# First norm of a diffusion layer: all modulation shifts as 2-column products on TensorE, scalings moved from GpSimd to VectorE

## The chip, the core and the metric

One core of a Trainium2 chip runs one layer of a hybrid recurrent backbone. The metric is the device time of one execution in microseconds (us). The engines named below are TensorE (PE in the rows, its weight loads PEld), VectorE (DVE), ScalarE (ACT), GpSimd (POOL) and SyncE (SP), which issues most transfers.

## The reference, cut to what matters

```python
def rmsnorm(x, w):
    y = x * lax.rsqrt(jnp.mean(x * x, axis=-1, keepdims=True) + EPS)
    return y * w
def modulate(xn, shift, scale):
    return xn * (1 + scale) + shift
mod_lat = jnp.split(silu(c) @ w_mod[l] + b_mod[l], N_MOD, axis=-1)
mod_ctx = jnp.split(silu(c_ctx) @ w_mod[l] + b_mod[l], N_MOD, axis=-1)
# first of three blocks; the same for the context tokens with mod_ctx
x = x + 0.5 * gate * swiglu(modulate(rmsnorm(x, norm1_w), shift, scale), ffn1_w1, ffn1_w2)
```

D_MODEL is 1024, there are 512 latent and 256 context tokens, and the hidden width is 2816. The whole layer is in float32. What is changed is the first `modulate(rmsnorm(...))` and its place beside the first products of `ffn1_w1`.

## The kernel before, in words

The activations lie transposed: 8 tiles `xa[k]` of 128 features by 768 tokens (columns 0 to 255 context, 256 to 767 latent). Every product of float32 matrices is made of three products of halves: a rounded high part (`xh`, `whi`) and a remainder (`xl`, `wlo`).

**Statistics.** ScalarE squares the 8 tiles, VectorE adds them, and TensorE sums over the partitions in `rms_sum` with matmuls whose stationary operand is a 128x128 block of squares and whose moving operand is one column of ones (`aux<-ones,six` in the rows). GpSimd takes the power, VectorE spreads it on a diagonal, and TensorE multiplies that with ones, so that the factor R stands in all partitions (`rms_spread`, `aux<-six,ones`).

**Modulation.** For tile k, scale and shift are 128 numbers each for latent and context. A scale is two VectorE reductions `mod_dot` of 128x1024 (one for `c`, one for `c_ctx`; `mod_scr` in the rows), then a small `TENSOR_SCALAR` into `a1`. A shift is one of two things. For tiles 5 and 7 (`SHIFT_V`) it is two more `mod_dot`. For the others it is 8 float32 matmuls on TensorE with the 128x2 `ccol` as stationary and 128 columns of weights as moving operand. This gives a row of 2x128, which ScalarE copies out of PSUM, TensorE transposes (`mm<-ident,row`), and ScalarE adds to the bias (`s1`). A float32 matmul stands in the records as two, so a shift is 16 records.

**Norm of a tile.** `scaled` multiplies the tile with R, on GpSimd for tiles 2, 4 and 6 (`ROOT_P`), on VectorE for the others. `norm_seg` then makes, for latent and context apart, `xh` and the full value in place on ScalarE, and `xl` as their difference on VectorE.

**Products.** `ffn1` makes the first two of 22 hidden tiles (each has a gate and an up half) as the norm proceeds: for each tile k there are four quarters, (hidden tile, half), of 6 matmuls each: three of 512 and three of 256 columns. After each quarter the generator `more(k)` is asked for one step. So what it yields stands between quarters in TensorE's order. TensorE, VectorE, ScalarE and GpSimd each run their instructions in the order written here (`ordered = True`); from the third hidden tile on a scheduler sets the order.

**Transfers.** SP issues in order; `fetch(k)` brings a tile of scale weights (512 KB) and one of shift weights. Shift weights and some `ffn1_w1` tiles share five buffers (`four`).

Of the kernel before, what the change touches and what calls it, by code (L numbers as in the profile page):

```python
# [7 lines left out]
F32 = mybir.dt.float32  # L8
F32R = mybir.dt.float32r
AF = mybir.ActivationFunctionType  # L10
ALU = mybir.AluOpType

P = 128
DM = 1024
KT = DM // P
# [11 lines left out]
CTX, LAT, LAT_A, LAT_B = (0, NC_), (NC_, NL), (NC_, 256), (NC_ + 256, 256)  # L27
ONES = [(m, 1) for m in range(KT)]
FOUR = [(0, 4)] + [(m, 1) for m in range(4, KT)]
CTX_MODS = (0, 1, 2, 3, 4)  # L30

SHIFT_V = (5, 7)
ROOT_P = (2, 4, 6)

# [33 lines left out]
class Space1:  # L70
# [14 lines left out]
    rows = lambda self, j, i: self.x[:, 2 * ((j + 2) % 4) + i, :]  # L85
# [13 lines left out]
class Builder:  # L99
# [1118 lines left out]
    def _build(self, st):  # L1218
        nc, tc, T = self.nc, self.tc, self.T
# [26 lines left out]
        with ExitStack() as f1:  # L1246
            p1 = lambda name, bufs=1, **kw: f1.enter_context(tc.tile_pool(name=name, bufs=bufs, **kw))
            space = self.space = Space1(self, p1("fp1"))
# [5 lines left out]
            xa = [xT[:, k, :] for k in range(KT)]  # L1254
            self.x, self.xc = [t[:, NC_:] for t in xa], [t[:, :NC_] for t in xa]
            crow = [space.quad(F32) for _ in range(2)]
            ccol = self.modp.tile([P, KT, 2], F32, name="ccol")
# [21 lines left out]
            for k in range(KT):  # L1279
                self.sq_add(S, k, xa[k], NT, "vvvvvvlv")()  # L1280
                if k in (0, 1, 3, 5):
                    r, q = parts[(k + 1) // 2]
                    nc.scalar.activation(self.cb[:, r, q * 512:q * 512 + 512], pcs[2 * r + q], AF.Silu)

            pc = self.ps.tile([P, 512], F32, name="mm")
            for _ in range(3):
                nc.tensor.matmul(pc, lhsT=self.ident, rhs=self.cb[:, 0, :512], start=True, stop=True)
            b1 = ct("b1", [P, KT])
            self.ts(b1, self.bmod[:, 1, :], 1.0, ALU.add)
            R = xT[:, KT, :]  # L1290
            a1, s1 = ct("a1", [P, KT, 2]), ct("s1", [P, KT, 2])

            def mod_dot(w, c, dst):
                scr = self.modp.tile([P, DM], mybir.dt.bfloat16, name="mod_scr", bufs=1)
                nc.vector.tensor_tensor_reduce(out=scr, in0=w, in1=self.cb[:, c, :], scale=1.0, scalar=0.0,
                                               op0=ALU.mult, op1=ALU.add, accum_out=dst)

            wms, wss = {}, {}

            def fetch(k):  # L1300
                wms[k] = self.modp.tile([P, DM], F32, name="wm", bufs=2) if k < 2 else self.tmp.tile([P, DM], F32)
                nc.sync.dma_start(out=wms[k], in_=T["w_mod"][KT + k])
                wss[k] = space.quad(F32)
                nc.sync.dma_start(out=wss[k], in_=T["w_mod"][k] if k in SHIFT_V else T["w_shift"][k])

            def shift(k):
                ws = wss.pop(k)
                if k in SHIFT_V:
                    for c in range(2):
                        mod_dot(ws, c, s1[:, k, c:c + 1])  # L1310
                    self.ts(s1[:, k, :], s1[:, k, :], self.bmod[:, 0, k:k + 1], ALU.add)
                    return
                pr = self.ps.tile([P, 512], F32, name="mm") if k < 2 else self.aux.tile([P, 512], F32, name="aux")
                for q in range(KT):
                    nc.tensor.matmul(pr[0:2, 0:P], lhsT=ccol[:, q, :], rhs=ws[:, q * P:(q + 1) * P],
                                     start=(q == 0), stop=(q == KT - 1))
                row = self.modp.tile([2, P], F32, name="row", bufs=2)
                nc.scalar.copy(out=row, in_=pr[0:2, 0:P])
                return row

            def shift_cols(k, row):
                if k in SHIFT_V:
                    return
                pt = self.ps.tile([P, 512], F32, name="mm") if k < 2 else self.aux.tile([P, 512], F32, name="aux")
                nc.tensor.transpose(out=pt[:, 0:2], in_=row, identity=self.ident[0:2, 0:2])
                nc.scalar.activation(s1[:, k, :], pt[:, 0:2], AF.Identity, bias=self.bmod[:, 0, k:k + 1])

            def scale(k):
                wm = wms.pop(k)
                for c in range(2):  # L1330
                    mod_dot(wm, c, a1[:, k, c:c + 1])
                self.ts(a1[:, k, :], a1[:, k, :], b1[:, k:k + 1], ALU.add, self.nw[:, 0, k:k + 1], ALU.mult)

            def norm_seg(k, w):
                lo, n = (LAT, CTX)[w]
                hi, x = self.xh[k][:, lo:lo + n], xa[k][:, lo:lo + n]
                kw = dict(scale=a1[:, k, w:w + 1], bias=s1[:, k, w:w + 1])
                nc.scalar.activation(hi, x, AF.Identity, **kw)
                nc.scalar.activation(x, x, AF.Identity, **kw)
                self.tt(self.xl[k][:, lo:lo + n], x, hi.bitcast(F32), ALU.subtract)  # L1340

            def scaled(k):
                (nc.gpsimd if k in ROOT_P else nc.vector).tensor_tensor(out=xa[k], in0=xa[k], in1=R, op=ALU.mult)

            rows = {}

            def more(k):

                for q in ((1, 2) if k == 0 else (k + 2,)):
                    if q >= KT:  # L1350
                        return
                    if q > 1:
                        if q + 2 < KT:
                            fetch(q + 2)
                        if q + 1 < KT:
                            scaled(q + 1)
                            scale(q + 1)
                    yield lambda: rows.__setitem__(q, shift(q)) if q not in SHIFT_V else None
                    yield lambda: (shift_cols(q, rows.get(q)), norm_seg(q, 0), norm_seg(q, 1),
                                   shift(q + 1) if q + 1 in SHIFT_V else None)  # L1360

            def w_raw(j, half):
                raw = space.quad(F32) if j else self.wp.tile([P, DM], F32, name="wraw", bufs=2)
                hi, lo = ([self.wp.tile([P, DM], F32R, name=n) for n in ("whi", "wlo")] if j + half < 2 else
                          [space.pair() for _ in range(2)])
                nc.sync.dma_start(out=raw, in_=T["f1w1"][j, half])
                return hi, lo, raw

            w_hi = lambda w: nc.scalar.activation(w[0], w[2], AF.Copy)
            w_lo = lambda w: self.tt(w[1], w[2], w[0].bitcast(F32), ALU.subtract)  # L1370
            fetch(0)
            w = [w_raw(0, 0), w_raw(0, 1), w_raw(1, 0), w_raw(1, 1)]
            fetch(1)
            accs = list(S.values())[::-1]
            mod_dot(wms[0], 0, a1[:, 0, 0:1])
            ms = [self.rms_sum([a[:, lo:lo + n] for a in accs], n) for lo, n in (LAT, CTX)]
            w_hi(w[0])
            w_hi(w[1])
            row = shift(0)
            mod_dot(wms[0], 1, a1[:, 0, 1:2])  # L1380
            dg = [self.rms_diag(m) for m in ms]
            self.ts(a1[:, 0, :], a1[:, 0, :], b1[:, 0:1], ALU.add, self.nw[:, 0, 0:1], ALU.mult)
            pR = [self.rms_spread(d) for d in dg]
            shift_cols(0, row)
            w_lo(w[0])
            segs = list(zip((LAT, CTX), pR))
            for (lo, n), r in segs:
                self.tt(xa[0][:, lo:lo + n], xa[0][:, lo:lo + n], r[:, :n], ALU.mult)
            w_lo(w[1])
            norm_seg(0, 0)  # L1390
            w_hi(w[2])
            norm_seg(0, 1)
            for (lo, n), r in segs:
                nc.scalar.copy(out=R[:, lo:lo + n], in_=r[:, :n])
            w_hi(w[3])
            w_lo(w[2])
            scale(1)
            self.tt(xa[1], xa[1], R, ALU.mult)
            w_lo(w[3])
            fetch(2)  # L1400
            fetch(3)
            scaled(2)
            scale(2)
            first = [[x[:2] for x in w[2 * q:2 * q + 2]] for q in range(2)]

            def late():
# [34 lines left out]
            def then(seg, b):  # L1441
                lo, n = seg

                def spill():
                    nc.sync.dma_start(out=xs[:, :, lo - NC_:lo - NC_ + n], in_=self.xT[:, :, lo - NC_:lo - NC_ + n])
                return self.seg_norm(seg, 3, b) + ([spill] if lo >= NC_ else [])
            self.ffn1(space, first, more, hook, mods, ahead, then)
            start = self.mixer_start(box["ws"])
        with ExitStack() as mx:
# [115 lines left out]
```

## Time and profile before

| | us |
|---|---|
| median of 3 runs (lowest to highest) | 1313.13 (1312.42 to 1314.64) |
| the profiled execution, its own time | 1315.44 |
| its span in the trace | 1313.6 |
| busy in it: TensorE, VectorE, ScalarE, GpSimd | 1287.5, 1012.3, 577.8, 56.5 |

The profiled execution's time lies 1.84 us over its span, and 2.31 us over the median of the runs. TensorE is busy 98% of the span. The granted clock of TensorE, PEclk, is given as a share of 2.4 GHz: 1.00 is the full level, 0.50 is 1.2 GHz.

### The profile page before, as it was taken

The numbers are of one execution on the slowest core, as the hardware profiler recorded it, in microseconds if no ns is written. First come the engines' busy times: TensorE is split into PE (matmuls) and PEld (weight loads), VectorE is DVE, ScalarE is ACT, GpSimd is POOL, SyncE is SP. The second block draws the span as 40 slices with busy tenths as digits, with TensorE's granted clock in tenths as the row PEclk, the third lists the DMA queues.
The fourth block names the chain that finished last, engine by engine and source line by source line (L and its number), as shares of the span: only waits on it lengthen the run. The fifth ranks groups of instructions, "written<-read, shape, count | busy, mean of one in ns | idle before, by whom it ended". The sixth has DMA issues, their size and how long they took to land.

```text
span 1313.6 us, 20542 instructions
## 1 busy us (share of the span) xinstructions
PE 1287.5 (98%) x8198; PEld 1180.6 (90%) x8198; DVE 1012.3 (77%) x1621; ACT 577.8 (44%) x992; POOL 56.5 (4%) x81
## 2 busy tenths in 40 slices
PE   8999999999999999999989999999999999999996
PEld 4689999999998888999978798889998999999996
DVE  5995878777779888767677867986578788888866
ACT  5562444444442222383457343444473444444434
POOL 2100000000000000110100000000000000000001
PEclk7999999999999999999989999999999999999998
DMA  8324443434687765413051101115224222233201
GB/s 330 122 88 155 134 150 121 137 136 149 211 279 236 267 212 195 148 44 120 2 146 48 65 33 49 64 49 171 87 99 142 97 96 97 102 108 105 104 17 65
DMA packets 48803, 163.60 MB, mean 125 GB/s; under 512 B 5554, under 2 KB 10034, under 8 KB 48708
## 3 DMA queue, kind: packets, MB, share of 16 engines
q1 hardware_dynamic: 46308, 150.50, 33.5%
q0 software_dynamic: 2400, 11.80, 2.8%
q8 instruction: 64, 1.05, 0.3%
q14 instruction: 31, 0.25, 0.1%
HBM read 149.39 MB, written 12.89 MB: 124 GB/s over the span
## 4 chain that ended last, share of the span: by engine, by line
PE 92%; DVE 3%; ACT 2%; issue 1%; DMA 1%; POOL 0%; SPq 0%; POOLq 0%; DVEq 0%
PE mm L56 71%; PE aux L56 21%; DVE mod_scr L56 1%; DMA x<-in_xT 0%; ACT xh L56 0%; DMA wraw<-in_wo 0%; DVE x L56 0%; ACT six L56 0%; ACT nm_y L56 0%; ACT x L56 0%; DVE wlo L56 0%; DVE xl L56 0%; ACT nm_t L56 0%; ACT whi L56 0%; POOL rms_acc L56 0%
## 5 line engine op out<-in xcount | busy, mean ns | idle before, releaser
L56 PE MATMUL mm<-xh,whi 128*128 128x256 f32 (+2 forms) x1072 | 345.6, 323 | 1.2 <-ACT xh L56 1.2
L56 PE MATMUL mm<-xh,wlo 128*128 128x256 f32 (+2 forms) x1072 | 342.6, 320 | 0.8 <-DVE wlo L56 0.8
L56 PE MATMUL mm<-xl,whi 128*128 128x256 f32 (+2 forms) x1000 | 323.8, 324 | 2.5 <-DVE xl L56 2.5
L56 PEld LDWEIGHTS mm<-xh,whi 128*128 128x128 f32 x1072 | 203.3, 190 | 14.3 <-issue 1.8
L56 PEld LDWEIGHTS mm<-xh,wlo 128*128 128x128 f32 x1072 | 203.5, 190 | 10.8 <-DVE wlo L56 1.0
L56 PE MATMUL mm<-six,whi 128*128 128x384 f32 (+1 forms) x752 | 209.2, 359 | 0.0
L56 PEld LDWEIGHTS mm<-xl,whi 128*128 128x128 f32 x1000 | 189.9, 190 | 14.5 <-DVE xl L56 4.3
L56 ACT ACTIVATE whi<-wraw 128x1024 fp32r<-128x1024 f32 x100 | 106.0, 1062 | 170.1 <-PE aux L56 90.9
L56 PEld LDWEIGHTS mm<-six,whi 128*128 128x128 f32 x752 | 135.6, 188 | 10.0
L56 PE MATMUL mm<-six,wlo 128*128 128x384 f32 (+1 forms) x376 | 134.4, 357 | 0.0
L56 DVE TENSOR_TENSOR wlo<-wraw,whi 128x1024 fp32r<-128x1024 f32 x100 | 121.8, 1220 | 10.5 <-ACT whi L56 10.4
L56 DVE CUSTOM_DVE_ANT_0 mod_scr<-wm,cb 128x1024 bf16<-128x1024 f32 x84 | 105.4, 1255 | 2.2 <-DMA wm<-in_w_mod 2.0
L56 PEld LDWEIGHTS mm<-six,wlo 128*128 128x128 f32 x376 | 70.6, 188 | 6.5
L56 DVE SCALAR_TENSOR_TENSOR x<-mm,mod_l,x 128x256 f32<-128x256 f32 (+1 forms) x88 | 51.9, 601 | 18.4 <-PE mm L56 18.3
L56 PE MATMUL aux<-ah,w2hi 128*128 128x512 f32 x160 | 64.1, 401 | 0.0
L56 ACT ACTIVATE whi<-four 128x1024 fp32r<-128x1024 f32 x37 | 39.2, 1061 | 56.1 <-PE mm L56 49.0
L56 PE MATMUL aux<-al,w2hi 128*128 128x512 f32 x160 | 63.1, 395 | 0.0
L56 DVE SCALAR_TENSOR_TENSOR x<-aux,mod_l,x 128x512 f32<-128x512 f32 x80 | 59.0, 745 | 5.2 <-PE aux L56 5.2
L56 DVE TENSOR_TENSOR wlo<-four,whi 128x1024 fp32r<-128x1024 f32 x37 | 45.3, 1224 | 22.7 <-ACT whi L56 22.7
L56 PE MATMUL aux<-ah,w2lo 128*128 128x512 f32 x160 | 62.4, 390 | 0.0
L56 PE MATMUL mm<-tl,whi 128*128 128x256 f32 x216 | 61.1, 283 | 0.0
L56 PE MATMUL aux<-six,whi 128*128 128x256 f32 x320 | 59.0, 282 | 0.0
(334 smaller groups left out, 2555.1 us busy)
## 6 DMA issues: line engine op xcount, KB each, us to landing
wraw<-in_f1w SPq DMA_DIRECT2D x62, 512.0 KB, 4.0
wm<-in_w_mod SPq DMA_DIRECT2D x58, 512.0 KB, 4.3
wraw<-in_f2w SPq DMA_DIRECT2D x44, 512.0 KB, 3.3
wraw<-in_wi SPq DMA_DIRECT2D x32, 512.0 KB, 3.3
w2raw<-in_f2w SPq DMA_DIRECT2D x22, 512.0 KB, 4.5
four<-h SPq DMA_DIRECT2D x22, 384.0 KB, 5.2
h<-x POOLq DMA_DIRECT2D x18, 384.0 KB, 3.0
wraw<-in_wo SPq DMA_DIRECT2D x8, 512.0 KB, 4.5
```

Of the source, the lines that this page charges most:

```text
L56: r = f(*a, **kw)
```

## The change

`SHIFT_V` and `ROOT_P` go. All eight shifts are made on TensorE with the operands exchanged: a 128x128 block of the weights is stationary and `ccol` moves, 2 columns wide. The result is already a column per partition, so the row, its copy and its transpose go. The shifts of tiles 1 to 7 stand between the quarters of tiles 0 and 1. All scalings with R are on VectorE. The dots of the next tile stand in front of each `xl`, which is one 768-column instruction from tile 1 on. A `keep_busy` of 4 idle matmuls (before: 3) stands ahead of the statistics, and another of 2 behind `rms_spread`. The order of the transfers changes with it.

```diff
-            pc = self.ps.tile([P, 512], F32, name="mm")
-            for _ in range(3):
-                nc.tensor.matmul(pc, lhsT=self.ident, rhs=self.cb[:, 0, :512], start=True, stop=True)
+            idle = self.ps.tile([P, 512], F32, name="mm")
+            def keep_busy(n):
+                for _ in range(n):
+                    nc.tensor.matmul(idle, lhsT=self.ident, rhs=self.cb[:, 0, :512], start=True, stop=True)
+            keep_busy(4)
...
             def shift(k):
                 ws = wss.pop(k)
-                if k in SHIFT_V:
-                    for c in range(2):
-                        mod_dot(ws, c, s1[:, k, c:c + 1])
-                    self.ts(s1[:, k, :], s1[:, k, :], self.bmod[:, 0, k:k + 1], ALU.add)
-                    return
-                pr = self.ps.tile([P, 512], F32, name="mm") if k < 2 else self.aux.tile([P, 512], F32, name="aux")
+                pr = self.aux.tile([P, 512], F32, name="aux")
                 for q in range(KT):
-                    nc.tensor.matmul(pr[0:2, 0:P], lhsT=ccol[:, q, :], rhs=ws[:, q * P:(q + 1) * P],
+                    nc.tensor.matmul(pr[:, 0:2], lhsT=ws[:, q * P:(q + 1) * P], rhs=ccol[:, q, :],
                                      start=(q == 0), stop=(q == KT - 1))
-                row = self.modp.tile([2, P], F32, name="row", bufs=2)
-                nc.scalar.copy(out=row, in_=pr[0:2, 0:P])
-                return row
...
+                nc.scalar.activation(s1[:, k, :], pr[:, 0:2], AF.Identity, bias=self.bmod[:, 0, k:k + 1])
...
+            def norm(k):
+                for out in (self.xh[k], xa[k]):
+                    for w in range(2):
+                        norm_act(k, w, out)
+                self.tt(self.xl[k], xa[k], self.xh[k].bitcast(F32), ALU.subtract)
...
             def scaled(k):
-                (nc.gpsimd if k in ROOT_P else nc.vector).tensor_tensor(out=xa[k], in0=xa[k], in1=R, op=ALU.mult)
+                self.tt(xa[k], xa[k], R, ALU.mult)
...
             def more(k):
...
+                q = k + 2
+                if k == 0:
+                    yield lambda: (shift(1), norm(1))
+                    yield lambda: (scaled(2), scale(2), fetch_shift(6), shift(2))
+                    yield lambda: (scaled(3), scale(3), norm(2), fetch_shift(7), shift(3))
+                    yield lambda: shift(4)
+                    return
+                if q + 1 < KT:
+                    scaled(q + 1)
+                    scale(q + 1)
+                if k == 1:
+                    yield lambda: shift(5)
+                    yield lambda: (norm(q), shift(6))
+                    yield lambda: shift(7)
+                elif q < KT:
+                    yield lambda: norm(q)
...
             pR = [self.rms_spread(d) for d in dg]
-            shift_cols(0, row)
+            keep_busy(2)
+            fetch(2)
+            fetch_shift(3)
+            fetch(3)
             w_lo(w[0])
+            mod_dot(wms[1], 0, a1[:, 1, 0:1])
```

The first place is TensorE beside the products of tile 0. In the names `xh,whi` is a moving and a stationary operand, `two` a weight half of the second hidden tile, `aux` and `mm` are PSUM banks. Before, the third quarter stands between a transpose and the shift of tile 2:

```order
L56 MATMUL mm<-ident,row 128x2
L56 MATMUL mm<-xh,whi 128x512
L56 MATMUL mm<-xl,whi 128x512
L56 MATMUL mm<-xh,wlo 128x512
L56 MATMUL aux<-xh,whi 128x256
L56 MATMUL aux<-xl,whi 128x256
L56 MATMUL aux<-xh,wlo 128x256
L56 MATMUL aux<-four,ccol 2x128 x8
```

Now it stands between two shifts with 2 moving columns, and so does each of the seven quarters from the second on:

```order
L53 MATMUL aux<-ccol,four 128x2 x8
L53 MATMUL mm<-xh,whi 128x512
L53 MATMUL mm<-xl,whi 128x512
L53 MATMUL mm<-xh,wlo 128x512
L53 MATMUL aux<-xh,whi 128x256
L53 MATMUL aux<-xl,whi 128x256
L53 MATMUL aux<-xh,wlo 128x256
L53 MATMUL aux<-ccol,four 128x2 x8
L53 MATMUL mm<-xh,two 128x512
```

The second place is VectorE ahead of the first product. `x<-x,aux` is tile 0 times R, `wlo` the low part of a weight, and the two rows named ISA are a dot and the reading of its sum. Before, the scaling of tile 0 follows the first `wlo`:

```order
L56 TENSOR_TENSOR wlo<-wraw,whi 128x1024
L56 TENSOR_TENSOR x<-x,aux 128x512
L56 TENSOR_TENSOR x<-x,aux 128x256
L56 TENSOR_TENSOR wlo<-wraw,whi 128x1024
L56 TENSOR_TENSOR xl<-x,xh 128x512
```

Now a dot of tile 1's scale weights (`wm`) stands in front of it:

```order
L53 TENSOR_TENSOR wlo<-wraw,whi 128x1024
L53 ISA mod_scr,a_155<-wm,cb 128x1024
L53 ISA a_155 128x1
L53 TENSOR_TENSOR x<-x,aux 128x512
L53 TENSOR_TENSOR x<-x,aux 128x256
L53 TENSOR_TENSOR wlo<-wraw,whi 128x1024
```

The dot came from behind `xl` of tile 0. From the third hidden tile on the engines' orders are those of before, apart from a few neighbours on VectorE and ScalarE that changed places.

## Rows read from the trace of the kernel before

**Rows 1.** The page, part 4: the chain that ended last, by engine.
```profile
PE 92%; DVE 3%; ACT 2%; issue 1%; DMA 1%; POOL 0%; SPq 0%; POOLq 0%; DVEq 0%
```
**Rows 2.** TensorE's timeline: start us, us, engine, line, what, count [wait].
```profile
25.02 0.49 PE L56 MATMUL mm<-xh,whi 128*128 128x512 f32 x1 [1.20 <-ACT xh L56]
...
28.40 0.58 PE L56 MATMUL mm<-xl,whi 128*128 128x256 f32 x1 [0.36 <-DVE xl L56]
...
51.31 1.91 PE L56 MATMUL aux<-four,ccol 128*2 128x128 f32 x16
...
54.39 0.22 PE L56 MATMUL aux<-ident,row 2*128 2x2 f32 x1
...
56.74 0.40 PE L56 MATMUL mm<-xh,whi 128*128 128x512 f32 x1
...
57.79 0.40 PE L56 MATMUL mm<-xh,whi 128*128 128x512 f32 x1
...
60.95 0.40 PE L56 MATMUL mm<-xh,whi 128*128 128x512 f32 x1
...
80.25 0.48 PE L56 MATMUL mm<-xh,six 128*128 128x512 f32 x1
```
**Rows 3.** VectorE and GpSimd from 28 to 47 us, timelines of each.
```profile
28.71 7.95 POOL L56 TENSOR_TENSOR x<-x 128x768 f32<-128x768 f32 x3 [8.58 <-ACT x L56]
...
29.40 2.83 DVE L56 CUSTOM_DVE_ANT_0 mod_scr<-wm,cb 128x1024 bf16<-128x1024 f32 x1
...
42.27 0.95 DVE L56 TENSOR_TENSOR x<-x 128x768 f32<-128x768 f32 x1
43.13 1.22 DVE L56 CUSTOM_DVE_ANT_0 mod_scr<-six,cb 128x1024 bf16<-128x1024 f32 x1
...
46.79 1.22 DVE L56 CUSTOM_DVE_ANT_0 mod_scr<-six,cb 128x1024 bf16<-128x1024 f32 x1
```
**Rows 4.** ScalarE and VectorE ahead of the first product, timelines of each.
```profile
17.34 1.06 ACT L56 ACTIVATE whi<-wraw 128x1024 fp32r<-128x1024 f32 x1 [3.20 <-DMA wraw<-in_f1w]
18.62 1.06 ACT L56 ACTIVATE whi<-wraw 128x1024 fp32r<-128x1024 f32 x1 [0.22 <-DMA wraw<-in_f1w]
...
23.27 1.02 DVE L56 TENSOR_TENSOR x<-x,aux 128x512 f32<-128x512 f32 x2 [1.36 <-PE aux L56]
```
**Rows 5.** Stretches: from:to, length, busy us of each engine, PEclk, DMA share, GB/s.
```profile
13.50:15.70 2.20, 1.51 (x14) 1.43 (x13) 1.53 (x3) 0.63 (x1) 0.00 (x0) 1.00 1.03 412
15.80:18.10 2.30, 2.30 (x12) 2.30 (x12) 0.70 (x3) 0.76 (x1) 1.03 (x1) 0.50 1.03 411
18.20:22.50 4.30, 4.30 (x18) 2.34 (x18) 3.64 (x7) 1.50 (x3) 1.61 (x1) 0.50 1.03 410
22.60:25.90 3.30, 1.72 (x6) 0.70 (x4) 2.20 (x4) 1.97 (x4) 0.00 (x0) 1.00 1.02 408
26.10:32.80 6.70, 5.83 (x22) 3.35 (x23) 5.29 (x6) 3.52 (x7) 4.09 (x2) 0.50 0.76 287
46.50:80.20 33.70, 33.70 (x198) 28.09 (x197) 30.36 (x55) 20.56 (x33) 0.00 (x0) 1.00 0.06 18
```
**Rows 6.** TensorE's timeline: PEclk is 0.50 in the first four, then returns (667.7 us).
```profile
15.18 3.07 PE L56 MATMUL aux<-ones,six 128*128 128x1 f32 x16 [0.69 <-DVE six L56]
...
29.12 3.58 PE L56 MATMUL mm<-four,ccol 128*2 128x128 f32 x16
...
664.33 0.41 PE L56 MATMUL mm<-whi,xh 128*128 128x256 f32 x1
664.54 0.41 PE L56 MATMUL mm<-wlo,xh 128*128 128x256 f32 x1
...
667.73 0.28 PE L56 MATMUL mm<-wlo,xh 128*128 128x256 f32 x1
```
**Rows 7.** TensorE's timeline: one-column sums at PEclk 1.00, later in the kernel.
```profile
550.58 1.40 PE L56 MATMUL aux<-ones,rms_acc 128*128 128x1 f32 x12
```
**Rows 8.** The tile `four`, 0 to 80 us: transfers, from issue to landing.
```profile
DMA to landing us min/median/max: 3.3/8.1/10.2
```

More of the change, by code (lines that the diff above doesn't have):

```diff
@@ L30 @@
 CTX_MODS = (0, 1, 2, 3, 4)
-SHIFT_V = (5, 7)
-ROOT_P = (2, 4, 6)
 MIXER = ("iv1 ck0 mq0 vals0 ck1 rows0 cq1 cols0 iv0 vals1 cq0 pair0 pair0 pair0 pair1 prep0 prep0 fin4 scan0 "
@@ L1298, in _build, with fetch, fetch_shift @@
             wms, wss = {}, {}
[L1300 to L1304, printed above, removed]
+            def fetch(*ks):
+                for k in ks:
+                    wms[k] = self.modp.tile([P, DM], F32, name="wm", bufs=2) if k < 2 else self.tmp.tile([P, DM], F32)
+                    nc.sync.dma_start(out=wms[k], in_=T["w_mod"][KT + k])
+            def fetch_shift(*ks):
+                for k in ks:
+                    wss[k] = space.quad(F32)
+                    nc.sync.dma_start(out=wss[k], in_=T["w_shift"][k])
             def shift(k):
                 ws = wss.pop(k)
-                if k in SHIFT_V:
-                    for c in range(2):
-                        mod_dot(ws, c, s1[:, k, c:c + 1])
-                    self.ts(s1[:, k, :], s1[:, k, :], self.bmod[:, 0, k:k + 1], ALU.add)
-                    return
-                pr = self.ps.tile([P, 512], F32, name="mm") if k < 2 else self.aux.tile([P, 512], F32, name="aux")
+                pr = self.aux.tile([P, 512], F32, name="aux")
                 for q in range(KT):
-                    nc.tensor.matmul(pr[0:2, 0:P], lhsT=ccol[:, q, :], rhs=ws[:, q * P:(q + 1) * P],
+                    nc.tensor.matmul(pr[:, 0:2], lhsT=ws[:, q * P:(q + 1) * P], rhs=ccol[:, q, :],
                                      start=(q == 0), stop=(q == KT - 1))
-                row = self.modp.tile([2, P], F32, name="row", bufs=2)
-                nc.scalar.copy(out=row, in_=pr[0:2, 0:P])
-                return row
[L1321 to L1326, printed above, removed]
+                nc.scalar.activation(s1[:, k, :], pr[:, 0:2], AF.Identity, bias=self.bmod[:, 0, k:k + 1])
             def scale(k):
@@ L1332, in scale, with norm_act @@
                 self.ts(a1[:, k, :], a1[:, k, :], b1[:, k:k + 1], ALU.add, self.nw[:, 0, k:k + 1], ALU.mult)
+            def norm_act(k, w, out):
+                lo, n = (LAT, CTX)[w]
+                nc.scalar.activation(out[:, lo:lo + n], xa[k][:, lo:lo + n], AF.Identity, scale=a1[:, k, w:w + 1],
+                                     bias=s1[:, k, w:w + 1])
             def norm_seg(k, w):
                 lo, n = (LAT, CTX)[w]
-                hi, x = self.xh[k][:, lo:lo + n], xa[k][:, lo:lo + n]
@@ L1337, in norm_seg @@
[L1337 to L1340, printed above, removed]
+                norm_act(k, w, self.xh[k])
+                norm_act(k, w, xa[k])
+                self.tt(self.xl[k][:, lo:lo + n], xa[k][:, lo:lo + n], self.xh[k][:, lo:lo + n].bitcast(F32), ALU.subtract)
+            def norm(k):
[3 more added lines that the diff above has]
+                self.tt(self.xl[k], xa[k], self.xh[k].bitcast(F32), ALU.subtract)
@@ L1342, in scaled @@
             def scaled(k):
-                (nc.gpsimd if k in ROOT_P else nc.vector).tensor_tensor(out=xa[k], in0=xa[k], in1=R, op=ALU.mult)
-            rows = {}
+                self.tt(xa[k], xa[k], R, ALU.mult)
             def more(k):
[L1349 to L1360, printed above, removed]
+                q = k + 2
@@ L1371, in _build @@
             fetch(0)
+            fetch_shift(0)
             w = [w_raw(0, 0), w_raw(0, 1), w_raw(1, 0), w_raw(1, 1)]
             fetch(1)
+            fetch_shift(1, 2)
             accs = list(S.values())[::-1]
@@ L1378, in _build @@
             w_hi(w[1])
-            row = shift(0)
+            shift(0)
             mod_dot(wms[0], 1, a1[:, 0, 1:2])
@@ L1388, in _build @@
                 self.tt(xa[0][:, lo:lo + n], xa[0][:, lo:lo + n], r[:, :n], ALU.mult)
+            wms.pop(0)
             w_lo(w[1])
@@ L1395, in _build @@
             w_hi(w[3])
+            mod_dot(wms[1], 1, a1[:, 1, 1:2])
+            wms.pop(1)
+            self.ts(a1[:, 1, :], a1[:, 1, :], b1[:, 1:2], ALU.add, self.nw[:, 0, 1:2], ALU.mult)
+            scaled(1)
             w_lo(w[2])
-            scale(1)
-            self.tt(xa[1], xa[1], R, ALU.mult)
             w_lo(w[3])
[L1400 to L1403, printed above, removed]
+            fetch(4, 5)
+            fetch_shift(4, 5)
+            fetch(6, 7)
             first = [[x[:2] for x in w[2 * q:2 * q + 2]] for q in range(2)]
```

## Prediction

> **What bounds the kernel now.** First the chain of work that ended last: 92% of it is TensorE [rows 1], so a change counts by what it does to TensorE's time. Then TensorE's timeline in the stretch that the change touches. The first product starts at 25.02 us, and the third hidden tile's first product at 80.25 [rows 2]: the stage is 55.2 us long. Behind it the engines' orders are those of before, so I price only this stage. A quarter takes 57.79 - 56.74 = 1.05 us and a tile of four 60.95 - 56.74 = 4.21 [rows 2], so eight tiles are 33.7 us of products. A shift takes 1.9 us and a transpose 0.2 [rows 2]; five of each stand in the stage: 10.5 us. That is 44.2 us of work at the full clock. The other 11 us are waits of tile 0, VectorE's late dots, and stretches at half clock.
>
> Third, the granted clock by stretches, where the reader is to look at PEclk beside the busy column [rows 5]. It is 1.00 in 13.5 to 15.7 us, which holds one-column sums, and 0.50 behind it, although TensorE is busy all of 15.8 to 18.1 with more such sums. It is still 0.50 in 18.2 to 22.5, which holds a shift with 128 moving columns and the wide products that spread R, and 1.00 behind that. It falls again behind 22.6 to 25.9, where TensorE is busy for half the time. At half clock from 26.1 us to 32.8 stands a shift of 128 moving columns, and it is 1.00 after it. From 46.5 us on, with products and such shifts, it stays 1.00.
>
> **The change, part by part.**
>
> *Scalings and dots on VectorE.* While GpSimd scales three tiles (28.71 to 36.66 us), a dot takes 2.83 us; alone it takes 1.22 [rows 3]. Two dots and a small operation are slowed there, about 4.5 us, which goes. The three scalings come to VectorE at 0.95 us each [rows 3], and four dots (tiles 5 and 7), 4.9 us, leave it. None of this is on TensorE's path later on: a tile costs VectorE one scaling, two dots and one difference, from 42.27 to 46.79 us, 4.5 us [rows 3]. That is 0.3 us more than TensorE's 4.21, but seven quarters and seven shifts now stand ahead of tile 2's products, over 20 us, and VectorE needs about 14 for what tile 2 waits for; the lead of 6 us covers six tiles. If that cover were gone, the cost would be 0.3 us a tile.
>
> *Start of the stage.* A dot of tile 1 now stands ahead of tile 0's scaling, which began at 23.27 us [rows 4]. Its weights are the fourth transfer behind the one that landed at 17.34; the next landed at 18.62 [rows 4], so 1.28 us apart, and these land at about 22.5. The dot ends at 23.7, and tile 0's scaling, its norm and the first product queue behind it: 0.4 us later. The last `xl` product of tile 0's first quarter starts at 28.8 instead of 28.40 [rows 2], and the quarter ends at 29.1. The 4 and 2 idle matmuls fall into time in which TensorE waits for these; at half clock the two behind the spreading may delay the first product, but it would wait for `xl` anyway (bounds 0 to 0.5 us, I take 0). ScalarE loses the row copies; VectorE's single 768-column `xl` costs no more than the two.
>
> *Transfers.* On SP the shift weights of tiles 4 and 5 now wait until the shifts of tiles 1 and 2 have read their buffers, and the scale weights of 6 and 7 wait behind them. They are needed three shifts and two or three quarters later, over 6 us at the full clock; a landing takes 3.3 us at best, 8.1 in the crowded start [rows 8]. I take 0, with 2 us as the upper end.
>
> *The shifts, at the full clock.* With the operands exchanged, the nearest rows are the one-column sums: a 128x128 stationary block for hardly any moving columns. Twelve records take 1.40 us [rows 7], so sixteen take 1.9: as much as the old form. So nothing is gained or lost per shift. Seven shifts stand in the stage instead of five (+3.8 us), and five transposes go (-1.0).
>
> *The sum at the full clock.* From 29.1 us: 31 quarters of 1.05 (32.6) and 7 shifts of 1.9 (13.3) end at 75.0, against 80.25: 5.2 us less.
>
> *The shifts and the clock.* Here I choose. From 29 us on TensorE's work is a shift, a quarter, a shift, a quarter, seven times, about two thirds of it shift at the full clock. The old shift kept company with a clock of 1.00, or stood just ahead of its return. The new shift's kin, the one-column sums, stood ahead of a fall and beside a clock that stayed down, with TensorE busy throughout [rows 5]. So I expect the clock to fall early in tile 0 and to be down for most of the fourteen pieces. The Trainium skill ("TensorE: Matmul & The Clock Gate", "What's actually happening") says that the gate follows how busy the engine has been; by it, with no gap in the shifts, the clock holds and the sum is the 5.2 us gain. The one-column stretch, busy 2.30 of 2.30 us at 0.50, speaks against reading "busy" as the profile's column does.
>
> At half clock a 256-column matmul takes 664.54 - 664.33 = 0.21 us [rows 6]. A quarter is 9 such units, 1.9 us, 0.85 over the full clock. A shift: sixteen sums took 3.07 us with the first half microsecond still fast, and the old shift 3.58 [rows 6]; I take 3.5, 1.6 over. A shift and a quarter lose 2.5 us. Bounds: none of the seven pairs, or all of them (17.5). I take six, 15.0 us. Behind them dense products at half clock must first bring the clock back. Where products alone did that, it took from before 664.3 to 667.7 us [rows 6], about 3.5 us, half of it lost: 1.7. The stage ends at 75.0 + 15.0 + 1.7 = 91.7 us, 11.5 later.
>
> The span becomes 1313.6 + 11.5 = 1325.1, with 1.84 around it 1326.9. The median of the runs is 2.31 below the profiled execution, so the forecast is 1324.6 us.
>
> **The rivals.**
>
> *The clock holds.* 1308 us (-5.2). For it: TensorE has no idle time between the pieces, and the idle matmuls stand ahead of them. Against it: the sums of 13.5 to 18.1 us. It decides if the full-speed quarters, a third of the time, are enough to hold 1.00; no stretch here shows that mix. Range 1306 to 1310.
>
> *The clock falls and returns in between.* The quarters at half clock are 1.9 us of every 5.4 and could bring it back for a while. With half the pairs slow: 3.5 x 2.5 = 8.7, without a final wait, less 5.2: 3.5 later, 1316.7 us. For it: wide products did bring it back at 22.6 us and at 667.7. Against it: it took longer dense stretches there. Range 1315 to 1321.
>
> *The change gains and loses the same.* Two pairs at half clock (5.0 us) cancel the gain: 1313 us, for instance if the fall comes only with the last shifts.
>
> **How the numbers follow.** Chances: clock down for most of the stage 0.40 (1321 to 1327), back in parts 0.23, cancelling 0.10, clock holds 0.27. A difference of 0.2%, 2.6 us, is about what this kernel's measurement can tell. So faster 0.27, same 0.10, slower 0.63. The range takes in the holding clock from below, 1307, since it has more than two chances in ten, and nearly all seven pairs from above, 1327.
>
> **What would show it.** In the trace after: PEclk in stretches between 26 and 70 us; the start of tile 2's first product (about 50 us if the clock holds, 65 if it is down); sixteen shift records in 1.9 us or in 3.5; no dot over 1.3 us; `xl` of tile 2 ready by 45 us, well ahead. Wrong would be: the clock stays at 1.00 beside the 2-column shifts, or TensorE waits for shift weights or for VectorE between tiles 1 and 3.

## The result and the profile after

The changed kernel takes 1326.56 us (median of 4 runs, 1324.85 to 1328.5) against 1313.54 before in the same set: ratio 1.0099, 95% interval 1.0085 to 1.0112. It is slower by 13 us; the forecast was 1324.6, in a range of 1307 to 1327.

The page of the profile after shows the loss without a place: TensorE is busy for 98% of the span as before, and only the second of the 40 slices of PEclk has fallen.

```profile
PE 1302.9 (98%) x8230; PEld 1201.6 (91%) x8230; DVE 1005.2 (76%) x1607; ACT 575.1 (43%) x988; POOL 48.7 (4%) x78
...
PEclk8599999999999999999989999999999999999998
```

Before, the last of these lines reads:

```profile
PEclk7999999999999999999989999999999999999998
```

The place is in the stretches (columns as in [rows 5]), cut where the granted clock changes:

```profile
13.20:19.90 6.70, 6.40 (x45) 5.32 (x45) 5.01 (x12) 3.21 (x5) 2.50 (x2) 1.00 1.03 411
20.00:23.30 3.30, 3.30 (x6) 1.69 (x5) 1.98 (x3) 0.00 (x0) 0.00 (x0) 0.50 1.02 408
23.50:26.70 3.20, 1.51 (x4) 0.36 (x2) 2.88 (x6) 2.26 (x3) 0.00 (x0) 1.00 1.03 410
26.90:67.60 40.70, 40.33 (x162) 37.46 (x163) 23.74 (x37) 14.78 (x30) 0.00 (x0) 0.50 0.35 134
67.90:92.30 24.40, 24.40 (x142) 21.39 (x141) 18.05 (x27) 12.34 (x19) 0.00 (x0) 1.00 0.06 22
```

The reader is to see the fourth line: TensorE is busy for 40.33 of 40.70 us, hardly waits, and has 1.2 GHz all that time. The third line is to be seen beside it: the clock fell at about 26.8 us, behind a stretch in which TensorE was busy for 1.51 of 3.20 us, and so ahead of the first of the seven shifts. The kernel before has the same fall at 26.1, and its clock was back at 32.8 [rows 5]. What this profile shows of the shifts is that the clock did not come back beside them; that it also falls beside them is seen in e9_dot_back_2col. TensorE's timeline shows what it does there:

```profile
25.27 0.50 PE L53 MATMUL mm<-xh,whi 128*128 128x512 f32 x1 [0.77 <-ACT xh L53]
...
29.25 3.41 PE L53 MATMUL aux<-ccol,four 128*128 128x2 f32 x16
...
32.51 0.77 PE L53 MATMUL mm<-xh,whi 128*128 128x512 f32 x1
...
34.58 3.41 PE L53 MATMUL aux<-ccol,four 128*128 128x2 f32 x16
...
66.58 0.63 PE L53 MATMUL mm<-xh,whi 128*128 128x512 f32 x1
...
67.81 0.28 PE L53 MATMUL mm<-xh,whi 128*128 128x256 f32 x1
...
92.31 0.46 PE L53 MATMUL mm<-xh,six 128*128 128x512 f32 x1
```

A shift of sixteen records takes 3.41 us and a quarter 34.58 - 32.51 = 2.07. Seven pairs, 5.33 us apart, run from 29.25 to 66.58, where tile 2's products begin. 1.2 us later the clock is back. The third hidden tile's first product comes at 92.31, 12.06 us later than before [rows 2]; the spans differ by 1325.5 - 1313.6 = 11.9. So the whole loss between the two profiles lies in this stage.

VectorE's timeline shows that it is not the cause:

```profile
22.48 1.22 DVE L53 CUSTOM_DVE_ANT_0 mod_scr<-wm,cb 128x1024 bf16<-128x1024 f32 x1 [1.32 <-DMA wm<-in_w_mod]
...
23.63 1.01 DVE L53 TENSOR_TENSOR x<-x,aux 128x512 f32<-128x512 f32 x2
...
43.59 0.95 DVE L53 TENSOR_TENSOR xl<-x,xh 128x768 fp32r<-128x768 f32 x1
...
56.71 0.96 DVE L53 TENSOR_TENSOR xl<-x,xh 128x768 fp32r<-128x768 f32 x1 [8.56 <-ACT x L53]
```

Tile 2's `xl` is ready at 44.5 us, 22 us before TensorE wants it. The long wait of tile 3's `xl` (8.56 us, on ScalarE, whose norms stand in order behind the slow shifts) is harmless: TensorE comes to tile 3 only at about 71.

### The profile page after: what moved, and what is told of

It reads as the page before. It is cut to its first block, busy times and chain, and to the rows that moved or that the text cites. A ratio compares the mean times of both kernels' runs of the same rounds, so it can differ in the third digit from the quotient of the medians.

```text
span 1325.5 us, 20586 instructions
## 1 busy us (share of the span) xinstructions
PE 1302.9 (98%) x8230; PEld 1201.6 (91%) x8230; DVE 1005.2 (76%) x1607; ACT 575.1 (43%) x988; POOL 48.7 (4%) x78
## 4 chain that ended last, share of the span: by engine, by line
PE 92%; ACT 2%; DMA 2%; DVE 2%; issue 1%; SPq 0%; POOL 0%; POOLq 0%; DVEq 0%; ACTq 0%
PE mm L53 70%; PE aux L53 22%; DMA wm<-in_w_mod 1%; DMA x<-in_xT 1%; DMA wraw<-in_wo 1%; ACT xh L53 1%; DVE x L53 0%; ACT nm_y L53 0%; ACT x L53 0%; SPq L1259 0%; ACT nm_t L53 0%; ACT whi L53 0%; DVE wlo L53 0%; POOL rms_acc L53 0%; DVE xl L53 0%
## 5 line engine op out<-in xcount | busy, mean ns | idle before, releaser
L53 DVE CUSTOM_DVE_ANT_0 mod_scr<-wm,cb 128x1024 bf16<-128x1024 f32 x84 | 102.3, 1218 | 2.2 <-DMA wm<-in_w_mod 2.0
```

What stands on the lines that cost most here:

```text
L53: r = f(*a, **kw)
```

## The experiments

Theory A: shifts with two moving columns let the clock fall, or keep it down, for the seven pairs, and without that the change would be a gain. Theory B: two more shifts on TensorE, and the order of the pieces, cost the time. The runs were made in three sets, each with the kernel before beside it: its median was 1312.98 in the first (e1 to e4), 1312.83 in the second (e5 to e8) and 1314.09 in the third (e9 to e11). Ratios are to that median, so runs of different sets are better compared by ratio.

### e1_old_form: the old operands at the new places

```diff
-  nc.tensor.matmul(pr[:, 0:2], lhsT=ws[:, q * P:(q + 1) * P], rhs=ccol[:, q, :], ...)
-  nc.scalar.activation(s1[:, k, :], pr[:, 0:2], ...)
+  nc.tensor.matmul(pr[0:2, 0:P], lhsT=ccol[:, q, :], rhs=ws[:, q * P:(q + 1) * P], ...)
+  nc.scalar.copy(out=rows[k], in_=pr[0:2, 0:P])
+  # cols(k), one quarter later: transpose of rows[k], then the activation into s1
```

> The changed kernel with the shifts' operands as before the change: two stationary columns, 128 moving ones, a row copy and a transpose, one quarter later. All eight stay on TensorE, in the places that the change gave them. Theory A (the clock: sixteen records with two moving columns let it fall, and all else is worth some 5 us): a shift and a quarter take 1.91 + 1.05 us in place of the 5.33 measured, seven pairs give back 16.6 us, less seven transposes of 0.22 (1.5): 1311.5 us, 1309 to 1314, granted clock 1.00 from 33 us on. Theory B (two more shifts on TensorE and the order of the pieces cost the time, whatever the operands): 1326 to 1328.

Measured: 1319.88 us, ratio 1.0052 (1.0035 to 1.0069): between the two, 8 us over theory A's figure. The stretches, ScalarE and TensorE at 40 to 45 us:

```profile
33.20:43.30 10.10, 7.48 (x52) 5.46 (x50) 6.01 (x9) 4.60 (x10) 0.00 (x0) 1.00 0.94 354
43.50:50.10 6.60, 5.53 (x22) 3.59 (x23) 6.42 (x14) 1.54 (x5) 0.00 (x0) 0.50 0.21 81
50.30:85.50 35.20, 35.20 (x216) 29.41 (x214) 25.91 (x35) 19.34 (x34) 0.00 (x0) 1.00 0.05 16
```

```profile
41.87 1.30 ACT L53 ACTIVATE xh<-x,s,a 128x512 fp32r<-128x512 f32 x2 [3.98 <-DVE a L53]
...
44.28 0.24 ACT L53 COPY row<-aux 2x128 f32<-2x128 f32 x1
```

```profile
44.57 0.26 PE L53 MATMUL aux<-ident,row 2*128 2x2 f32 x1 [3.89 <-ACT row L53]
```

The old form brings a wait that the new one does not have. The row copy of shift 3 stands on ScalarE behind tile 2's norm, which waits 3.98 us for VectorE's dots; TensorE's transpose waits 3.89 us for the copy, and within that idle time the clock falls to 0.50, for 6.8 us. On both sides of it, from 33.4 to 43.4 us and from 50.2 on, the clock is at 1.00 beside these shifts. So A is supported, its sum was not: 3.9 of wait and half of 6.8 are 7.3 us that it left out.

### e2_pad128: two columns repeated to 128

```diff
-  nc.tensor.matmul(pr[:, 0:2], lhsT=ws[:, q * P:(q + 1) * P], rhs=ccol[:, q, :], ...)
+  cols = ccol[:, q, :].rearrange("p (o r) -> p o r", o=1).broadcast_to([P, 64, 2])
+  nc.tensor.matmul(pr[:, 0:128].rearrange("p (o r) -> p o r", r=2), lhsT=ws[:, q * P:(q + 1) * P], rhs=cols, ...)
```

> The changed kernel, with the two moving columns of each shift repeated to 128 (the other 126 results are not used). Stationary blocks, places and what follows stay. Theory A in the form 'few moving columns': the clock holds, a shift takes 1.9 to 2.1 us, the seven pairs 7 x 3.0: 1309 us, 1308 to 1312. Theory A in the form 'loads of whole stationary blocks, each used once': the clock falls as before, a shift takes 3.4 to 3.8 us: 1326 to 1330. Theory B (order and number of pieces): 1326 to 1328, with the clock at 1.00 and waits on TensorE in their place.

Measured: 1311.36 us, ratio 0.9991 (0.9981 to 1.0000), 15 us less than the changed kernel (14 by the ratios). Stretches and TensorE:

```profile
28.80:32.10 3.30, 3.30 (x18) 3.30 (x17) 3.26 (x6) 0.85 (x1) 0.00 (x0) 0.50 0.38 150
32.20:76.40 44.20, 43.52 (x284) 39.24 (x283) 38.64 (x58) 24.39 (x42) 0.00 (x0) 1.00 0.29 108
```

```profile
28.83 3.54 PE L53 MATMUL aux<-ccol,four 128*128 128x128 f32 x16
...
33.26 1.95 PE L53 MATMUL aux<-ccol,four 128*128 128x128 f32 x16
...
36.10 1.95 PE L53 MATMUL aux<-ccol,four 128*128 128x128 f32 x16
...
42.60 2.05 PE L53 MATMUL aux<-ccol,four 128*128 128x128 f32 x16 [0.68 <-ACT s L53]
```

Same stationary blocks, same places, same number of records: only the moving columns differ, and the clock, down when the first shift starts, is back at its end (32.2 us) and stays. That excludes theory B, and it excludes the weight loads alone as the cause. Against the kernel before, the gain is 1.6 us, and the interval of its ratio reaches 1.0000.

### e3_spread: the same shifts, one to a tile

```diff
   yield lambda: (shift(1), norm(1))
-  yield lambda: (scaled(2), scale(2), fetch_shift(6), shift(2))
-  yield lambda: (scaled(3), scale(3), norm(2), fetch_shift(7), shift(3))
-  yield lambda: shift(4)
+  yield lambda: (scaled(2), scale(2), fetch_shift(6))
+  yield lambda: (scaled(3), scale(3), shift(2), norm(2), fetch_shift(7))
...
-  if k == 1:
-      yield lambda: shift(5)
-      yield lambda: (norm(q), shift(6))
-      yield lambda: shift(7)
-  elif q < KT:
-      yield lambda: norm(q)
+  if q < KT:
+      yield lambda: (shift(q), norm(q))
```

> The changed kernel with two shifts in tile 0 and one in each later tile, operands as changed: the same TensorE work, only spread. Theory A: four quarters behind each shift hold or restore the clock; at most the two pairs of tile 0 run slow (2 x 2.35) with a return of 1.7: 1309 to 1315 us. If a single shift of two moving columns lets the clock fall for the quarters behind it, each of six tiles loses 1 to 3 us: up to 1325. Theory B (work on TensorE sets the time): same work, 1326.

Measured: 1312.73 us, ratio 1.0000 (0.9991 to 1.0010). The profiled execution is the slowest of the ten, 1316.55.

```profile
31.90:48.80 16.90, 16.90 (x65) 15.35 (x65) 15.20 (x24) 7.32 (x14) 0.00 (x0) 0.50 0.71 248
48.90:81.90 33.00, 33.00 (x214) 29.76 (x212) 22.22 (x34) 16.40 (x27) 0.00 (x0) 1.00 0.06 17
```

```profile
29.01 1.84 PE L53 MATMUL aux<-ccol,four 128*128 128x2 f32 x16
...
33.80 3.40 PE L53 MATMUL aux<-ccol,four 128*128 128x2 f32 x16
...
41.05 3.41 PE L53 MATMUL aux<-ccol,four 128*128 128x2 f32 x16
...
50.66 1.84 PE L53 MATMUL aux<-ccol,four 128*128 128x2 f32 x16
```

The two-column shift itself is as fast as its padded form at the full clock (1.84 us). The first three shifts have two quarters between them, and there the clock fell and was down for 17 us. The later ones have four quarters between them; there it came back and stayed. Again the same TensorE work in another time.

### e4_filler: more work, less time

```diff
+  for _ in range(5 if k else 0):
+      nc.tensor.matmul(pr, lhsT=first[0][0][0][:, :P], rhs=self.xh[0][:, NC_:], start=True, stop=True)
   for q in range(KT):
       nc.tensor.matmul(pr[:, 0:2], ...)
```

> The changed kernel with five idle products of 512 columns ahead of each of the seven shifts beside the products (results not used). They are 35 x 2 x 0.107 = 7.5 us of extra TensorE work at the full clock. Theory A: the wide products hold the clock up, 1309 + 7.5 = 1316.5 us, faster than the changed kernel although it does more. If they do not hold it, they cost 14.9 at half clock: 1341. Theory B: 1326.6 + 7.5 = 1334.

Measured: 1317.24 us, ratio 1.0037 (1.0018 to 1.0056). Theory A said 1316.5. The stretch, then the first idle products and the shift behind them:

```profile
25.60:56.10 30.50, 29.79 (x193) 25.81 (x192) 23.83 (x35) 13.25 (x25) 0.00 (x0) 1.00 0.54 198
```

```profile
29.16 1.31 PE L53 MATMUL aux<-xh,whi 128*128 128x512 f32 x5
30.31 1.84 PE L53 MATMUL aux<-ccol,four 128*128 128x2 f32 x16
```

With 35 useless products, 1.15 us for each five, the kernel is 9 us faster than the changed kernel without them (8 by the ratios), because all seven pairs run at 1.00. The products did not do it every time: one of the nine runs took 1328.19 us at a mean granted clock of 0.982, the others 1315.7 to 1317.9 at 0.991 or more. That run has no profile.

### e5_pad_order: the norm behind the small operation

```diff
-  yield lambda: (scaled(3), scale(3), norm(2), fetch_shift(7), shift(3))
-  yield lambda: shift(4)
+  yield lambda: (scaled(3), scale(3), fetch_shift(7), shift(3))
+  yield lambda: (shift(4), norm(2))
```

(on top of e2_pad128)

> The changed kernel with 128 moving columns in each shift, and tile 2's norm issued behind shift 4 instead of ahead of shift 3, so that ScalarE's small operation of shift 3 no longer stands behind a norm that waits for VectorE's dots. If that queue is what TensorE waited 0.68 us for ahead of shift 5 in the padded kernel: that wait goes, 1310.7 us against 1311.4, third hidden tile's first product at 75.7 instead of 76.42. If the wait only moves to another shift: 1311 to 1312.

Measured: 1310.5 us, ratio 0.9979 (0.9970 to 0.9989). ScalarE's operation of shift 3 now stands ahead of the norm:

```profile
40.90 0.26 ACT L53 ACTIVATE s<-aux,cst 128x2 f32<-128x2 f32 x1 [2.58 <-PE aux L53]
41.06 1.29 ACT L53 ACTIVATE xh<-x,s,a 128x512 fp32r<-128x512 f32 x2
```

The wait of 0.68 us is gone and none has taken its place. The third hidden tile starts at 75.45, against 76.42 in e2_pad128. In the medians the two differ by 0.9 us, and the intervals of their ratios overlap.

### e6_no_gpsimd: only the scalings, in the kernel before

```diff
-ROOT_P = (2, 4, 6)
+ROOT_P = ()
```

> The kernel before, with its three scalings on VectorE instead of GpSimd and nothing else changed. Reading of the prediction: the two dots beside GpSimd's work take 1.22 instead of 2.83 us, tile 1 is ready some 4 us earlier, TensorE's waits of 0.82, 1.04 and 0.78 us between 38 and 42 us go, and perhaps the stretch at half clock behind them (1.7): 1308.7 to 1310.5 us. Rival: the scalings lengthen VectorE's queue by 2.9 us and TensorE waits there: 1313 to 1316.

Measured: 1309.33 us, ratio 0.9975 (0.9966 to 0.9985). In VectorE's timeline a dot that took 2.83 us [rows 3] now reads:

```profile
29.83 1.22 DVE L56 CUSTOM_DVE_ANT_0 mod_scr<-wm,cb 128x1024 bf16<-128x1024 f32 x1
```

Of TensorE's waits between 30 and 76 us one of 0.56 is left, and the clock is at 1.00 from 33.84 on. So this part of the change alone is worth 3.5 us in the medians, within the 1308.7 to 1310.5 expected. The rival (a net loss by VectorE's longer queue) is excluded.

### e7_swap_only: only the operands, in the kernel before

```diff
-  nc.tensor.matmul(pr[0:2, 0:P], lhsT=ccol[:, q, :], rhs=ws[:, q * P:(q + 1) * P], ...)
-  # row copy; transpose and activation in shift_cols
+  nc.tensor.matmul(pr[:, 0:2], lhsT=ws[:, q * P:(q + 1) * P], rhs=ccol[:, q, :], ...)
+  nc.scalar.activation(s1[:, k, :], pr[:, 0:2], AF.Identity, bias=self.bmod[:, 0, k:k + 1])
```

> The kernel before with the shifts' operands exchanged (weights stationary, two moving columns) and no row copy or transpose, at the old places: shift 0 ahead of the products, two in tile 0, one each in tiles 1, 2 and 4; tiles 5 and 7 on VectorE as before. Theory A: the exchange alone lets the clock fall or stay down in tiles 0 and 1, where three shifts stand close, some 10 to 17 us at 0.50 instead of the 10 of before: 0 to 4 us more, less 1.1 for five transposes and 1.0 for a wait on a row copy: 1311 to 1315, and 1.00 behind tile 2. Theory B: operands are indifferent: 1311, clock as before.

Measured: 1314.93 us, ratio 1.0018 (1.0009 to 1.0027), within A's range and at its upper end; theory B's 1311 is excluded.

```profile
15.80:36.20 20.40, 18.42 (x66) 14.93 (x66) 15.45 (x21) 8.00 (x12) 10.33 (x5) 0.50 0.79 306
...
39.70:49.80 10.10, 7.93 (x30) 7.25 (x31) 9.92 (x19) 6.13 (x11) 0.00 (x0) 0.50 0.67 263
50.00:80.20 30.20, 30.20 (x186) 26.87 (x186) 26.92 (x48) 16.94 (x26) 0.00 (x0) 1.00 0.05 18
```

```profile
41.87 0.79 PE L56 MATMUL mm<-xl,whi 128*128 128x512 f32 x1 [2.24 <-DVE xl L56]
```

Even without the new places the exchange does not pay: the clock is down for 30 us of the first 50. The profile does not split how much of that is the shifts' and how much comes of a wait of 2.24 us for tile 1's `xl` at 41.87.

### e8_dot_back and e11_best_again: tile 1's first dot behind tile 0

```diff
-  mod_dot(wms[1], 0, a1[:, 1, 0:1])          # ahead of tile 0's scaling
   ...
   w_hi(w[3])
+  mod_dot(wms[1], 0, a1[:, 1, 0:1])
   mod_dot(wms[1], 1, a1[:, 1, 1:2])
```

(on top of e5_pad_order; e11_best_again is the same kernel again)

> The padded, reordered kernel with the first dot of tile 1 moved back behind tile 0's differences, as in the kernel before. If the early dot's wait for its weights delays tile 0 as the prediction says: tile 0's scaling starts 0.4 us earlier (23.3 instead of 23.6) and so does the first product, 0.4 us less than the padded, reordered kernel; tile 1's scaling comes 1.2 us later, with TensorE two shifts ahead of it. If the dot is hidden: same time, or some tenths more where tile 1 is late.

> The padded kernel with tile 2's norm later and the dot back, a second time, beside the two others of this set: 1308.2 us (1307 to 1309.5). If the first run's gain came of a chance early in the clock's course, its profile shows a first product at 25 us and the median lies near 1310.5.

Measured: 1308.18 us, ratio 0.9964 (0.9951 to 0.9976), and 1307.07 us, ratio 0.9951 (0.9936 to 0.9965). This version beats both kernels: 4.7 and 7.0 us under the one before in the same set, some 18 to 19 under the changed one. VectorE in e5_pad_order, for comparison, and in the first profile, then TensorE and the stretch in the second:

```profile
22.52 1.23 DVE L53 CUSTOM_DVE_ANT_0 mod_scr<-wm,cb 128x1024 bf16<-128x1024 f32 x1 [0.47 <-DMA wm<-in_w_mod]
...
23.67 1.01 DVE L53 TENSOR_TENSOR x<-x,aux 128x512 f32<-128x512 f32 x2
```

```profile
20.85 1.01 DVE L53 TENSOR_TENSOR x<-x,aux 128x512 f32<-128x512 f32 x2
```

```profile
15.21 2.73 PE L53 MATMUL aux<-ones,six 128*128 128x1 f32 x24
...
23.18 0.50 PE L53 MATMUL mm<-xh,whi 128*128 128x512 f32 x1
...
26.90 1.95 PE L53 MATMUL aux<-ccol,four 128*128 128x128 f32 x16
```

```profile
14.00:71.90 57.90, 55.93 (x356) 48.31 (x355) 52.59 (x82) 32.13 (x53) 2.50 (x2) 1.00 0.51 195
```

Tile 0's scaling starts at 20.85 us, not at 23.3 as expected, and the first product at 22.49 and 23.18 instead of 25.32 in e5_pad_order. The dot's price is 2.3 us in the medians of one set (1310.5 - 1308.2), not 0.4. The intervals of the two ratios touch, but five of the seven runs with the dot back are faster than all ten with it early. Of the 2.8 us between the two profiles 1.1 arose ahead of the dot: `wlo` in front of it starts at 20.83 us in e5_pad_order and at 19.71 in e8_dot_back.

### e9_dot_back_2col: the same move in the changed kernel

The diff is that of e8_dot_back, on the changed kernel with its two columns.

> The changed kernel with two moving columns, and only the first dot of tile 1 back behind tile 0's differences. If the early dot costs what the prediction says: 0.4 us less, 1326.2. If it costs what the padded pair of kernels differ by in their medians (1310.5 - 1308.2): 2.3 us less, 1324.3, with the first product ahead of 25.0 us and tile 0's scaling waiting for the spread R instead of for a transfer. The stretch at half clock over seven pairs stays either way, and the pairs take 5.3 us each.

Measured: 1323.66 us, ratio 1.0073 (1.0058 to 1.0088). The median is 2.9 us under that of the changed kernel, but the two ratios' intervals still touch, and the profile gives the gain another place. VectorE, TensorE and the stretches:

```profile
23.77 0.69 DVE L53 TENSOR_TENSOR x<-x,aux 128x512 f32<-128x512 f32 x1 [1.60 <-PE aux L53]
```

```profile
29.14 1.84 PE L53 MATMUL aux<-ccol,four 128*128 128x2 f32 x16
...
31.98 3.27 PE L53 MATMUL aux<-ccol,four 128*128 128x2 f32 x16
```

```profile
25.40:32.10 6.70, 5.95 (x34) 4.10 (x33) 5.18 (x9) 4.82 (x8) 0.00 (x0) 1.00 0.71 281
32.20:66.20 34.00, 34.00 (x139) 31.87 (x139) 22.48 (x34) 12.84 (x25) 0.00 (x0) 0.50 0.33 124
```

In this execution the spreading of R ran at half clock, so the scaling came no earlier than in the changed kernel (23.77 and 23.63 us), and the first product came at 26.16, not ahead of 25.0 as expected. The gain is that the clock held for the first shift. It then fell at about 32.1 us, behind that shift and one quarter. The profile of e4_filler has nearly the same rows up to 29.1 us and wide products ahead of each shift, and there the clock did not fall. So in these executions two-column shifts did not only keep a low clock down, they also let a high one fall. The long stretch at 0.50 stayed, as expected.

### e10_no_idle: without the two idle products behind the spreading

```diff
   pR = [self.rms_spread(d) for d in dg]
-  keep_busy(2)
```

(on top of e8_dot_back)

> The padded kernel with tile 2's norm later and the dot back, without the two idle products behind the spread of R. Prediction's term (they cost nothing, 0 to 0.5 us, TensorE waits there anyway): 1308.2 us, 1307.7 to 1308.4. Rival: TensorE is then idle for longer ahead of the first products and the clock is down for one stretch more in tile 0: 1309 to 1311 us, with a half-clock stretch of 7 us instead of 3.4 in the profile.

Measured: 1308.83 us, ratio 0.9958 (0.9944 to 0.9972), beside 1307.07 for the same kernel with them, whose interval overlaps. It lies between the two expectations (up to 1308.4, and from 1309). The profile has the rival's stretch, 0.50 from 23.8 to 30.6 us, but one profile does not say how often it comes. It stays open whether the two products help by up to 2 us; they do no harm that could be measured.

## Why the prediction was right, step by step

**The clock.** This step carried the forecast and held: the clock was down for all seven pairs. The Trainium skill ("TensorE: Matmul & The Clock Gate", "What's actually happening") has the gate follow how busy the engine has been; the trace disagrees if busy is read as the profile's column does, since 40.33 of 40.70 us stood at 0.50. That the moving columns decide here is shown by e2_pad128, that work of another kind holds the clock by e4_filler. Two things were not as written. The fall came early in tile 0, but in its first quarter, ahead of the first of these shifts, so it was not theirs; what they did was to keep the clock down. And the one-column sums, from which the direction was taken, are weak evidence: in the changed kernel itself 24 of them stood at 1.00 from 14.7 us on, and the clock fell only at 20. That they pointed the right way was in part luck, and the range, 1307 to 1327, held both outcomes.

Sizes: I took six slow pairs of seven, it was all seven. A shift took 3.41 us (3.5 taken), a quarter 2.07 (1.9). A pair at half clock took 5.33 us and at the full clock 31.98 - 29.14 = 2.84 (e9_dot_back_2col), so it lost 2.49 (2.5). The return cost less than the 1.7 taken: 1.2 us of products at half clock, 0.6 lost. 7 x 2.49 + 0.6 = 18.0 against 16.7 in the prediction. At 2.84 a pair the sum at the full clock ends at 74.3 us and not at 75.0, so the two errors partly cancel: 92.3 measured, 91.7 forecast.

**The sum at the full clock.** Forecast: the stage ends at 75.0 us, a gain of 5.2. The changed order with padded shifts (e5_pad_order) ends it at 75.45, with one shift still slow, so the end was well priced, and the shift of 1.9 us, estimated from one-column sums [rows 7], was 1.84. The gain in the medians was smaller: 1.6 us in e2_pad128 and 2.3 in e5_pad_order, although the scalings' move away from GpSimd alone is worth 3.5 (e6_no_gpsimd). The sum was set against one execution of the kernel before that was 2.31 us over its median, and the forecast took the same 2.31 off the changed kernel. How much of the difference comes of this and how much of the early dot was not split.

**The start.** Here a term was mis-sized. In the two profiles it is right: the first quarter ends at 29.25 (29.1 forecast), and tile 0's scaling starts 0.36 us later than in [rows 4]. But the 0.4 was read from one execution in which the spreading of R ran at half clock and so came late anyway. The early dot waits for a transfer that lands at about 22.5 us and so holds the scaling at 23.6 or 23.7 (changed kernel, e5_pad_order). Without it the scaling starts at 23.77 us where the clock is down (e9_dot_back_2col) and at 20.85 or 21.54 where it is up (e8_dot_back, e11_best_again). So the dot costs nothing in some executions and 2 to 3 us in others.

**Transfers, idle products, VectorE's lead.** All at nothing, as forecast: from 30 us on TensorE waits for nothing in the stage, no dot takes over 1.23 us, and tile 2's `xl` came at 44.5 us, just inside the 45 named.

**The rivals.** A clock that holds was worth 1308; the padded kernels, which hold it from 32 us on, take 1310.5 to 1311.4, and reach 1307 to 1309 only with the early dot moved back. The return in parts did not come with one quarter between two shifts, nor with two, but did with four (e3_spread). The cancelling case did not come.

## What to carry to other kernels

Before many matmuls with a few moving columns are put beside dense products, look at the granted clock of a stretch in which the kernel already runs such matmuls, and in more than one execution; a full busy column does not show it (here 40.33 of 40.70 us at half clock). If they must stand there, repeat their columns (here from 2 to 128, which cost at most 0.1 us a shift) or set them far apart (here four quarters, 4.2 us). Before a wait is put ahead of the critical engine's first input, price it in the execution in which that input comes earliest, not in the one that was profiled.

## What the runs showed of the hardware that was not expected

Sixteen records with 128 moving columns take 1.95 us, with 2 columns 1.84, both at the full clock. Even these 0.11 us do not delay what follows: from one shift to the next, with a quarter between, it is 36.10 - 33.26 = 2.84 us with 128 columns (e2_pad128) and 31.98 - 29.14 = 2.84 with 2 (e9_dot_back_2col). TensorE's weight loads are busy throughout beside them (3.30 of 3.30 us in the first stretch of e2_pad128), which points to the loads as what sets the pace; no run changed them alone.

The clock's course in the first 30 us is not the same from one execution to the next. The same kernel had 0.50 from 26.3 to 29.7 us in one profile (e8_dot_back) and 1.00 from 14 to 652 us in the other (e11_best_again); in that one the 24 one-column sums stood at the full clock, while in [rows 5] they stood ahead of a fall. So the sums, from which the forecast took its direction, show that a fall can come beside such matmuls, and not that it must. The runs of the padded kernels spread over 2.7 to 4.5 us; that the clock's course is the reason is not shown.
